# Two conditional blocks per expert pair moved ahead of the pair's own products, and one common block for all further places

## The chip, the cores and the metric

One NeuronCore of a Trainium2 chip runs the whole network in one launch. The metric is the device time of one execution in microseconds (us); less is better. Work is spread over TensorE (matrix products, PE in the profile), VectorE (DVE), ScalarE (ACT) and GpSimd (POOL); SyncE (SP) issues the loads of weights. Each engine has a sequencer of its own that takes its instructions in order, and engines wait for each other and for loads by semaphores.

## The reference

The network is two blocks of two layers each, on 256 tokens of width 1024. Twice, in the first block, a layer ends with a mixture of experts: 16 experts with a hidden width of 512, in 4 groups, of which each token takes the best two experts of the best group.

```python
h = rms_norm(x, norm2_g[layer]) * (1.0 + sc2) + sh2
x = x + g2 * grouped_moe(h, router_w, router_b, exp_w_gate[layer],
                         exp_w_up[layer], exp_w_down[layer])
```

An expert computes `(silu(h @ gate) * (h @ up)) @ down` for its tokens, weighted by the router's score. How many tokens an expert gets is known only when the router has run, so the kernel has to branch on the chip.

## The kernel before

`moe(l)` runs an expert stage, once for layer 0 and once for layer 1. It handles the experts in eight pairs, p = 0 to 7. Each expert has 64 places in its pair's own products: `up(p)` gathers the rows of its tokens with a one-hot matrix (`gather`, PE tile `ph`, evacuated by ACT into `hg`; one gather serves two pairs, so it is made in the even pairs), multiplies with the gate weights (`pg`) and the up weights (`pu`), scatters the pair before (`py`), and turns the hidden rows (`hT`, copied by DVE into `hidT`); `down(p)` multiplies with the down weights (`po`).

Tokens beyond 64 places go through `more_up` and `more_down`, 32 places of each expert at a time. Round r = 1 holds places 65 to 96 and rounds 2 to 6 the rest. The counts of a stage (`cnti`, the larger of a pair's two) are loaded into registers of PE, DVE and ACT, and `tc.If(count > ...)` makes each of them compare and branch for itself. An engine that skips a block jumps behind it and lifts the semaphores there, in EVENT_SEMAPHORE instructions, by what the skipped instructions would have lifted them.

For the pairs 2 to 6 the program reads: `up(p)`; a first block with `more_up` of round 1 and, nested in it, both halves of rounds 2 to 6; `down(p)`; a second block with `more_down` of round 1. The pair 7 has one nest in place of the first block, with all rounds for itself and for the pairs 0 and 1. Only this nest fetches weights again, so only there SP branches too; the other blocks use the weights `W` of their pair, which are still in place. With this input one block is entered: in layer 0 the first block of the pair 3 (round 1), with its second block. Everything else is skipped: in a stage five first blocks and the nest of pair 7, or in layer 0 four and the nest.

Weights come in pieces of 1 MB, twelve for a pair (four of gate, up and down each), into a ring of 17 slots (`self.turn`). SP issues them in order. A slot may be filled anew when the last instruction of the program that reads it, entered or skipped, is done. At most eight loads are under way: each one waits for the eighth before it.

The order of the instructions on each engine is made by a scheduler, but only within the stretch between two branches; the products of `gather`, `pg`, `pu` and `po` keep the order in which they are written.

Of the kernel before, what the change touches and what calls it, by code (L numbers as in the profile page):

```python
# [11 lines left out]
F32 = mybir.dt.float32  # L12
# [9 lines left out]
P = 128  # L22
D = 1024
S = 256
# [95 lines left out]
class Net:  # L120
# [1093 lines left out]
    def moe(self, l):  # L1214
# [4 lines left out]
        with self.phase(f"moe{l}", MOE_RING, True) as mp:  # L1219
# [95 lines left out]
            for p in range(FIRST):  # L1315
                V.tensor_tensor(cnt[:, 7:8], cnt[:, p:p + 1], cnt[:, 7:8], op=ALU.max)
# [42 lines left out]
            def places(oh, p, r, keep=True):  # L1359
# [7 lines left out]
                if keep:  # L1367
                    Sm = kept[:, 3 if r else 2, :]
                    ws = mp.tile([P, 1], F32, tag="ws", name="ws", bufs=3)
                else:  # L1370
                    Sm = self.sp.tile([P, 256], F32R, tag="e1", name="Sma")
                    ws = mp.tile([P, 1], F32, tag="wsa", name="wsa")
# [6 lines left out]

            def up(p, W):  # L1380

                new = p % 2 == 0
                if new:
                    hg = self.sp.tile([P, KD, 256], F32, tag="xn", name="hg", bufs=1)
                    self.first = hot((p, p + 1), 0, 64), hg
                    gather(*self.first, 0, 4)
# [22 lines left out]
                V.tensor_copy(hidT, pt)  # L1409
                return hidT, Sm, ws  # L1410
# [43 lines left out]
            def more_up(p, r, W, hidT, keep):  # L1454
# [18 lines left out]
                Sm, ws = places([twice[:, t].rearrange("p c s -> p (c s)") for t in range(2)], p, r, keep)  # L1473
# [9 lines left out]
            def more_down(p, W, hidT, Sm, ws, own=False):  # L1483
# [13 lines left out]
                if own:  # L1497
                    eh, el = (self.sp.tile([P, 512], F32R, tag="e1", name="eoa") for i in range(2))
                else:
                    eo = self.htp.tile([P, 4, 512], F32R, tag="hThi", name="eo")  # L1500
                    eh, el = eo[:, 0, :], eo[:, 1, :]
# [6 lines left out]
            def rounds(p, r, W):  # L1508

                if r < 7:  # L1510
                    with tc.If(count > 32 + 32 * r):
                        if p == 7 and r == 1:
                            self.spare = [self.slot([P, 2048]) for i in range(4)]
                        for pp, w in [(p, W)] + [(e, None) for e in range(FIRST if p == 7 else 0)]:
                            hidT = self.sp.tile([P, 4, 64], F32, tag="gt", name="hidTa")
# [821 lines left out]
```

## Time and profile before

| | |
|---|---|
| median of 3 runs | 1672.31 us (1666.22 to 1675.63) |
| profiled execution | 1670.24 us, span from first to last instruction 1668.4 us |
| granted TensorE clock, mean of the span | 0.965 |
| layer 0's experts, first gather to the end of the last `po` | 210.2 to 489.8 us |
| layer 1's experts, the same | 647.4 to 909.6 us |
| largest groups of idle PE in them | 50.8 us ahead of `po`, 6.4 us ahead of `hT` |
| weights of one stage | 96 loads of 1 MB, by SP |

The profiled execution is 2.1 us under the median of the runs; the stages lie in it at the times of the table, which count from the span's start. Within a stage the pairs follow each other in `pg`, `pu`, `hT`, `po`, and idle time of PE stands in the rows beside the group that came after it, with what ended it.

### The profile page before, as it was taken

The numbers are of one execution on the slowest core, as the hardware profiler recorded it, in microseconds if no ns is written. First come the engines' busy times: TensorE is split into PE (matmuls) and PEld (weight loads), VectorE is DVE, ScalarE is ACT, GpSimd is POOL, SyncE is SP. The second block draws the span as 40 slices with busy tenths as digits, with TensorE's granted clock in tenths as the row PEclk, the third lists the DMA queues.
The fourth block names the chain that finished last, engine by engine and source line by source line (L and its number), as shares of the span: only waits on it lengthen the run. The fifth ranks groups of instructions, "written<-read, shape, count | busy, mean of one in ns | idle before, by whom it ended". The sixth has DMA issues, their size and how long they took to land. (4 is left out here: it accounts for less than half of the span.)

```text
span 1668.4 us, 24040 instructions
## 1 busy us (share of the span) xinstructions
PE 1548.3 (93%) x9485; PEld 1109.3 (66%) x9485; DVE 855.4 (51%) x1624; ACT 651.3 (39%) x1341; POOL 123.1 (7%) x170
## 2 busy tenths in 40 slices
PE   6999999888879999998788899999999999999998
PEld 3766534333339975433233688789999897889997
DVE  4755512221238984222113776765555777755555
ACT  3435321110126553111012554664444766654443
POOL 0330200000000002000000200210000212110000
PEclk9999999998989999999899999999999999999999
DMA  9998999789977889999896743355555443454640
GB/s 358 350 315 285 367 392 354 272 303 338 344 256 231 277 317 348 397 338 384 326 340 246 230 108 94 107 183 190 190 174 172 162 135 119 143 186 158 219 155 26
DMA packets 225779, 412.58 MB, mean 247 GB/s; under 512 B 7704, under 2 KB 91312, under 8 KB 225616
## 3 DMA queue, kind: packets, MB, share of 16 engines
q1 hardware_dynamic: 223040, 403.46, 68.6%
q0 software_dynamic: 2304, 6.98, 1.3%
q8 instruction: 98, 1.61, 0.4%
q14 instruction: 65, 0.53, 0.1%
q10 hardware_dynamic: 272, 0.00, 0.0%
HBM read 409.35 MB, written 1.06 MB: 246 GB/s over the span
## 5 line engine op out<-in xcount | busy, mean ns | idle before, releaser
L229 DVE TENSOR_TENSOR hl<-w,hl 128x1024 fp32r<-128x1024 f32 x280 | 335.1, 1229 | 55.2 <-ACT hl L228 54.8
L228 ACT CAST hl<-w 128x1024 fp32r<-128x1024 f32 x280 | 280.3, 1045 | 32.0 <-DMA w<-in_even_w_in 19.8
L1427 PE MATMUL po<-w,hidT 128*64 128x512 f32 x512 | 138.0, 700 | 50.8 <-PEq L1541 21.6
L380 PE MATMUL pgu<-hThi,hl 128*128 128x256 f32 x640 | 180.9, 283 | 0.0
L382 PE MATMUL pgu<-hThi,hl 128*128 128x256 f32 x640 | 180.8, 283 | 0.0
L381 PE MATMUL pgu<-hTlo,hl 128*128 128x256 f32 x640 | 180.7, 282 | 0.0
L380 PE MATMUL lin<-hl,hThi 128*128 128x256 f32 (+2 forms) x480 | 158.6, 334 | 1.3 <-ACT hThi L551 0.6
L381 PE MATMUL lin<-hl,hThi 128*128 128x256 f32 (+2 forms) x480 | 153.2, 320 | 2.8 <-DVE hl L229 2.7
L382 PE MATMUL lin<-hl,hTlo 128*128 128x256 f32 (+2 forms) x480 | 152.6, 319 | 0.2 <-DVE hTlo L557 0.2
L1427 PEld LDWEIGHTS po<-w,hidT 128*64 128x64 f32 x512 | 45.2, 161 | 133.4 <-issue 127.7
L1396 PE MATMUL pu<-w,hg 128*64 128x512 f32 x512 | 124.6, 595 | 0.0
L381 PEld LDWEIGHTS pgu<-hTlo,hl 128*128 128x128 f32 x640 | 122.4, 191 | 1.8
L380 PEld LDWEIGHTS pgu<-hThi,hl 128*128 128x128 f32 x640 | 122.4, 191 | 1.7
L382 PEld LDWEIGHTS pgu<-hThi,hl 128*128 128x128 f32 x640 | 122.4, 191 | 0.1
L1396 PE MATMUL pg<-w,hg 128*64 128x512 f32 x512 | 115.3, 597 | 2.9 <-PEq L1545 1.7
L1442 ACT CAST eo<-of 128x512 fp32r<-128x512 f32 x32 | 19.8, 617 | 223.6 <-DVE of L1439 223.3
L380 PEld LDWEIGHTS lin<-hl,hThi 128*128 128x128 f32 x480 | 92.6, 193 | 16.3 <-issue 7.9
L1439 DVE SCALAR_TENSOR_TENSOR of<-po,ws,gate 128x512 f32<-128x512 f32 x32 | 23.9, 748 | 149.6 <-PE po L1427 149.6
L381 PEld LDWEIGHTS lin<-hl,hThi 128*128 128x128 f32 x480 | 92.5, 193 | 11.8 <-DVE hl L229 4.3
L382 PEld LDWEIGHTS lin<-hl,hTlo 128*128 128x128 f32 x480 | 92.3, 192 | 7.6 <-issue 1.7
L1417 DVE TENSOR_TENSOR x<-x,py 128x512 f32<-128x512 f32 x68 | 42.8, 683 | 99.3 <-PE py L1415 99.3
L1396 PEld LDWEIGHTS pu<-w,hg 128*64 128x64 f32 x512 | 38.2, 137 | 71.9 <-issue 70.3
(547 smaller groups left out, 2934.2 us busy)
## 6 DMA issues: line engine op xcount, KB each, us to landing
w<-in_exp_w_gate SPq DMA_DIRECT2D x64, 1024.0 KB, 16.2
w<-in_exp_w_down SPq DMA_DIRECT2D x64, 1024.0 KB, 15.4
w<-in_exp_w_up SPq DMA_DIRECT2D x64, 1024.0 KB, 10.7
w<-in_ada_w SPq DMA_DIRECT2D x48, 1024.0 KB, 7.5
w<-in_ffn_wg SPq DMA_DIRECT2D x22, 1024.0 KB, 5.5
w<-in_ffn_wu SPq DMA_DIRECT2D x22, 1024.0 KB, 7.3
w<-in_ffn_wd SPq DMA_DIRECT2D x22, 1024.0 KB, 8.8
w<-in_even_w_in SPq DMA_DIRECT2D x14, 1024.0 KB, 10.2
```

The costliest lines, as they stand in the source:

```text
L228: pin(self.nc.scalar.copy(w[:, 0], src))
L229: pin(self.nc.vector.tensor_tensor(w[:, 1], src, w[:, 0].bitcast(F32), op=ALU.subtract))
L380: pin(mm(out, lh, rh, start=start, stop=False))
L381: pin(mm(out, lh, rl, start=False, stop=False))
L382: pin(mm(out, ll, rh, start=False, stop=stop))
L1396: pin(mm(pp[64 * j:64 * j + 64, :], hg[:, k, q][:, 64 * j:64 * j + 64], w[j][k // 4][:, k % 4, :], start=k == 0, stop=k == KD - 1, tile_po ...
L1417: V.tensor_tensor(xs, xs, py, op=ALU.add)
L1427: pin(mm(po[c][64 * j:64 * j + 64, :], hidT[:, k, 64 * j:64 * j + 64], W[2][j][k // 2][:, k % 2, 512 * c:512 * c + 512], start=k == 0, sto ...
L1439: V.scalar_tensor_tensor(of, po[c], ws, gate[:, cs], op0=ALU.mult, op1=ALU.mult)
L1442: nc.scalar.copy(eh[c], of)
```

## The change

The blocks of the pairs 2 to 7 now hold round 1 alone. The first one, `more_up`, stands ahead of `up(p)` (behind `down` of the pair before), and the second one, `more_down`, between `up(p)` and `down(p)`. All rounds from 2 on, of all pairs, and round 1 of the pairs 0 and 1, form one nest ahead of the pair 7, on a count `left` that is the largest of all, with 32 added for the pairs 0 and 1. It fetches every weight itself, into the four slots that the down weights of pair 7 get after it, so those are fetched behind the nest; the first loads of the next layer follow them, ahead of the pair's own products. The gather for the next two pairs is made at the end of `up` of the pairs 1, 3 and 5 (`prepare`). `Sm` always lies in `kept` now.

```diff
@@ -1312,8 +1312,8 @@
             cnt = mp.tile([1, 8], F32, name="cnt")
             V.tensor_reduce(cnt, pc.rearrange("p (a b) -> p a b", b=2), axis=AX.X, op=ALU.max)
 
-            for p in range(FIRST):
-                V.tensor_tensor(cnt[:, 7:8], cnt[:, p:p + 1], cnt[:, 7:8], op=ALU.max)
+            V.tensor_scalar(cnt[:, 0:FIRST], cnt[:, 0:FIRST], 32.0, None, op0=ALU.add)
+            V.tensor_reduce(cnt[:, 0:1], cnt, axis=AX.X, op=ALU.max)
             cnti = mp.tile([1, 8], I32, name="cnti")
             V.tensor_copy(cnti, cnt)
 
@@ -1356,7 +1356,7 @@
                         nc.scalar.activation(hg[:, k, :], ph[:, b, :], AF.Identity,
                                              scale=A[:, k:k + 1], bias=B[:, k:k + 1])
 
-            def places(oh, p, r, keep=True):
+            def places(oh, p, r):
 
                 pS = self.bank([P, 256], name="pS")
                 pw = self.bank([P, 16], name="pw")
@@ -1364,11 +1364,10 @@
                     self.tr(pS[:, 128 * t:128 * t + 128], oh[t].bitcast(F32))
                     mm(pw, oh[t], ch[:, t, :], start=t == 0, stop=False)
                     mm(pw, oh[t], cl[:, t, :], start=False, stop=t == 1)
-                if keep:
-                    Sm = kept[:, 3 if r else 2, :]
+                Sm = kept[:, 3 if r else 2, :]
+                if not r:
                     ws = mp.tile([P, 1], F32, tag="ws", name="ws", bufs=3)
                 else:
-                    Sm = self.sp.tile([P, 256], F32R, tag="e1", name="Sma")
                     ws = mp.tile([P, 1], F32, tag="wsa", name="wsa")
                 nc.scalar.copy(Sm, pS)
                 m = 32 if r else 64
@@ -1377,13 +1376,17 @@
                     nc.scalar.copy(ws[m * i:m * i + m, :], pw[m * i:m * i + m, e:e + 1])
                 return Sm, ws
 
+            def prepare(p, k1=KD):
+
+                hg = self.sp.tile([P, KD, 256], F32, tag="xn", name="hg", bufs=1)
+                self.first = hot((p, p + 1), 0, 64), hg
+                gather(*self.first, 0, k1)
+
             def up(p, W):
 
-                new = p % 2 == 0
+                new = p == 0
                 if new:
-                    hg = self.sp.tile([P, KD, 256], F32, tag="xn", name="hg", bufs=1)
-                    self.first = hot((p, p + 1), 0, 64), hg
-                    gather(*self.first, 0, 4)
+                    prepare(0, 4)
                 oh, hg = self.first
                 q = slice(128 * (p % 2), 128 * (p % 2) + 128)
                 pg = self.bank([P, 512], name="pg")
@@ -1407,6 +1410,8 @@
                     self.tr(pt[:, k, :], hd[:, 128 * k:128 * k + 128])
                 hidT = self.sp.tile([P, 4, P], F32, tag="e2", name="hidT")
                 V.tensor_copy(hidT, pt)
+                if p in (1, 3, 5):
+                    prepare(p + 1)
                 return hidT, Sm, ws
 
             def scatter(py, t, c, Sm, eh, el):
@@ -1451,7 +1456,7 @@
                     if l:
                         self.split_ahead(PRE)
 
-            def more_up(p, r, W, hidT, keep):
+            def more_up(p, r, W, hidT):
 
 
                 oh = hot((p,), 32 + 32 * r, 32)
@@ -1470,7 +1475,7 @@
                 twice = self.sp.tile([P, 2, 2, 64], F32R, tag="gt", name="ohd")
                 for t in range(2):
                     V.tensor_copy(twice[:, t], oh[t].unsqueeze(1).to_broadcast([P, 2, 64]))
-                Sm, ws = places([twice[:, t].rearrange("p c s -> p (c s)") for t in range(2)], p, r, keep)
+                Sm, ws = places([twice[:, t].rearrange("p c s -> p (c s)") for t in range(2)], p, r)
                 hd = self.sp.tile([P, 512], F32, tag="gt", name="hda")
                 nc.scalar.copy(hd, pp)
                 pt = self.bank([P, 4, P], name="hT")
@@ -1480,7 +1485,7 @@
                 V.tensor_tensor(hidT, hidT, pt[:, :, 64:128], op=ALU.mult)
                 return Sm, ws
 
-            def more_down(p, W, hidT, Sm, ws, own=False):
+            def more_down(p, W, hidT, Sm, ws):
                 po = self.bank([P, 512], name="po")
                 w = W[2] if W else weights("exp_w_down", 256, p, self.spare)
                 for k in range(4):
@@ -1494,28 +1499,21 @@
                     h = slice(64 * c, 64 * c + 64)
                     V.scalar_tensor_tensor(of[h, :], po[h, :], ws[h, :], gate[h, 512 * c:512 * c + 512], op0=ALU.mult,
                                            op1=ALU.mult)
-                if own:
-                    eh, el = (self.sp.tile([P, 512], F32R, tag="e1", name="eoa") for i in range(2))
-                else:
-                    eo = self.htp.tile([P, 4, 512], F32R, tag="hThi", name="eo")
-                    eh, el = eo[:, 0, :], eo[:, 1, :]
+                eh, el = (self.sp.tile([P, 512], F32R, tag="e1", name="eoa") for i in range(2))
                 self.split(of, eh, el)
                 for c in range(2):
                     h = slice(64 * c, 64 * c + 64)
                     for t in range(2):
                         scatter(self.bank([P, 512], name="py"), t, c, Sm[h, 128 * t:128 * t + 128], eh[h, :], el[h, :])
 
-            def rounds(p, r, W):
-
-                if r < 7:
-                    with tc.If(count > 32 + 32 * r):
-                        if p == 7 and r == 1:
-                            self.spare = [self.slot([P, 2048]) for i in range(4)]
-                        for pp, w in [(p, W)] + [(e, None) for e in range(FIRST if p == 7 else 0)]:
-                            hidT = self.sp.tile([P, 4, 64], F32, tag="gt", name="hidTa")
-                            Sm, ws = more_up(pp, r, w, hidT, False)
-                            more_down(pp, w, hidT, Sm, ws)
-                        rounds(p, r + 1, W)
+            def rounds(r):
+
+                with tc.If(left > 32 + 32 * r):
+                    for rr, pp in [(1, e) for e in range(FIRST if r == 2 else 0)] + [(r, e) for e in range(8)]:
+                        hidT = self.sp.tile([P, 4, 64], F32, tag="e2", name="hidTa")
+                        more_down(pp, None, hidT, *more_up(pp, rr, None, hidT))
+                    if r < 6:
+                        rounds(r + 1)
 
             engines = (mybir.EngineType.PE, mybir.EngineType.DVE, mybir.EngineType.Activation)
 
@@ -1528,27 +1526,28 @@
                 return t[0::2], t[1::2]
 
             for p in range(8):
-                W = [weights("exp_w_gate", 512, p), weights("exp_w_up", 512, p), weights("exp_w_down", 256, p)]
-                if p >= FIRST:
-                    count = nc.values_load(cnti[0:1, p:p + 1], min_val=0, max_val=S,
-                                           engines=engines + (mybir.EngineType.SP,) * (p == 7))
-                own = up(p, W)
-                if p < FIRST:
-                    down(W, *own)
-                elif p < 7:
-
-                    hidT = self.sp.tile([P, 4, 64], F32, tag="e2", name="hidTb")
-                    with tc.If(count > 64):
-                        Sm, ws = more_up(p, 1, W, hidT, True)
-                        rounds(p, 2, W)
-                    down(W, *own)
-                    with tc.If(count > 64):
-                        more_down(p, W, hidT, Sm, ws, True)
-                else:
-                    rounds(p, 1, W)
+                W = [weights("exp_w_gate", 512, p), weights("exp_w_up", 512, p)]
+                self.spare = [self.slot([P, 2048]) for i in range(4)]
+                if p == 7:
+                    left = nc.values_load(cnti[0:1, 0:1], min_val=0, max_val=2 * S,
+                                          engines=engines + (mybir.EngineType.SP,))
+                    rounds(2)
+                W.append(weights("exp_w_down", 256, p, self.spare))
+                if p == 7:
                     self.turn, self.nload = [self.ring] * RING, 0
                     self.resume()
-                    down(W, *own, True)
+                if p < FIRST:
+                    down(W, *up(p, W))
+                    continue
+
+                count = nc.values_load(cnti[0:1, p:p + 1], min_val=0, max_val=S, engines=engines)
+                hidT = self.sp.tile([P, 4, 64], F32, tag="e2", name="hidTb")
+                with tc.If(count > 64):
+                    Sm, ws = more_up(p, 1, W, hidT)
+                own = up(p, W)
+                with tc.If(count > 64):
+                    more_down(p, W, hidT, Sm, ws)
+                down(W, *own, p == 7)
 
 
     def mixer1(self):
```

What the built program makes of it, engine by engine. First PE in layer 0, from the turning of pair 2's hidden rows to its second block; before, `hT` on line 183 is followed by the branch on line 1541, the last four rows of whose block (round 6) stand ahead of `po`:

```order
L1489 MATMUL po<-w,hidTa 32x512 x16
L1414 MATMUL py<-eo,Sma 128x512 x4
L1415 MATMUL py<-eo,Sma 128x512 x4
L1511 UNCONDITIONAL_BRANCH x6
L1541 UNCONDITIONAL_BRANCH
L1427 MATMUL po<-w,hidT 64x512 x16
L1545 COMPARE_AND_BRANCH
L1489 MATMUL po<-w,hidTb 32x512 x16
L1414 MATMUL py<-eoa,kept 128x512 x4
L1415 MATMUL py<-eoa,kept 128x512 x4
L1545 UNCONDITIONAL_BRANCH x2
```

and now the same place, where 1548 is the line of the second block and 1545 that of pair 3's first one:

```order
L183 MATMUL hT<-kt,hd 128x128 x4
L1548 COMPARE_AND_BRANCH
L1494 MATMUL po<-w,hidTb 32x512 x16
L1419 MATMUL py<-eoa,kept 128x512 x4
L1420 MATMUL py<-eoa,kept 128x512 x4
L1548 UNCONDITIONAL_BRANCH x2
L1432 MATMUL po<-w,hidT 64x512 x16
L1545 COMPARE_AND_BRANCH
```

The jump between `hT` and `po` skips 24 matrix instructions as these rows count them (16 + 4 + 4), where it skipped 74 + 5 x 98 = 564, and the jump behind `po` skips 74 where it skipped 24. The nest ahead of pair 7 holds 980 + 4 x 784 = 4116 (before, pair 7's held 6 x 294 = 1764).

Second, PE at pair 3 of layer 0. Before, the gather (`ph<-kept`) follows the second block of line 1545:

```order
L1427 MATMUL po<-w,hidT 64x512 x16
L1545 COMPARE_AND_BRANCH
L1489 MATMUL po<-w,hidTb 32x512 x16
L1414 MATMUL py<-eoa,kept 128x512 x4
L1415 MATMUL py<-eoa,kept 128x512 x4
L1545 UNCONDITIONAL_BRANCH x2
L1352 MATMUL ph<-kept,xh 128x256
L1352 MATMUL ph<-kept,xl 128x256
```

and now its 32 products end ahead of the second block, line 1548:

```order
L1352 MATMUL ph<-kept,xl 128x256
L1548 COMPARE_AND_BRANCH
L1494 MATMUL po<-w,hidTb 32x512 x16
L1419 MATMUL py<-eoa,kept 128x512 x4
L1420 MATMUL py<-eoa,kept 128x512 x4
L1548 UNCONDITIONAL_BRANCH x2
L1432 MATMUL po<-w,hidT 64x512 x16
L1545 COMPARE_AND_BRANCH
```

The gather moved from behind `po` to between `hT` and `po`. Third, SP's loads for pair 7 of layer 0, before:

```order
L221 DMA w<-in_exp_w_gate 128x4x512 x3
L221 DMA w<-in_exp_w_up 128x4x512
L1541 UNCONDITIONAL_BRANCH
L221 DMA w<-in_exp_w_up 128x4x512 x3
L221 DMA w<-in_exp_w_down 128x2x1024 x4
L1545 UNCONDITIONAL_BRANCH
L1511 COMPARE_AND_BRANCH
```

and now, ahead of the nest:

```order
L221 DMA w<-in_exp_w_up 128x4x512 x3
L1548 UNCONDITIONAL_BRANCH
L221 DMA w<-in_ada_w 128x4x512
L1511 COMPARE_AND_BRANCH
```

and behind it:

```order
L1511 UNCONDITIONAL_BRANCH x6
L221 DMA w<-in_exp_w_down 128x2x1024 x4
L1545 UNCONDITIONAL_BRANCH
L221 DMA w<-in_odd_w_in 128x8x256 x5
L1548 UNCONDITIONAL_BRANCH
```

The four down loads moved behind the nest, and in layer 0 one load of another weight (`ada_w`) came ahead of it.

## Rows read from the trace of the kernel before

**Rows 1.** Page, part 2: 40 slices of the span (41.7 us each), tenths.

```profile
PEclk9999999998989999999899999999999999999999
DMA  9998999789977889999896743355555443454640
```

**Rows 2.** Groups by line, PE: out<-in, count | busy us, mean ns | idle before, releasers.

```profile
L1427 PE MATMUL po<-w,hidT 128*64 128x512 f32 x512 | 138.0, 700 | 50.8 <-PEq L1541 21.6 <-DMA w<-in_exp_w_up 13.9 <-DVEq L1511 7.3
L183 PE MATMUL hT<-kt,hd 128*128 128x128 f32 x64 | 10.5, 286 | 6.4 <-DVE hd L1404 6.4
L1396 PE MATMUL pg<-w,hg 128*64 128x512 f32 x512 | 115.3, 597 | 2.9 <-PEq L1545 1.7 <-ACT hg L1356 0.7
```

**Rows 3.** Timeline of PE, pieces: start, duration, line, count, idle before and releaser.

```profile
333.36 8.78 PE L1427 MATMUL po<-w,hidT 128*64 128x512 f32 x32 [3.55 <-PEq L1511]
...
650.91 3.88 PE L1396 MATMUL pg<-w,hg 128*64 128x512 f32 x16
...
692.92 0.66 PE L183 MATMUL hT<-kt,hd 128*128 128x128 f32 x4
695.02 7.09 PE L1427 MATMUL po<-w,hidT 128*64 128x512 f32 x32 [1.44 <-DVE hidT L1409]
...
758.65 9.74 PE L1427 MATMUL po<-w,hidT 128*64 128x512 f32 x32 [5.76 <-PEq L1541]
...
867.86 9.75 PE L1427 MATMUL po<-w,hidT 128*64 128x512 f32 x32 [3.42 <-PEq L1541]
```

**Rows 4.** Sequencer instructions of line 1541: durations in ns, least/median/most.

```profile
L1541 PEldq COMPARE_BRANCH  x10: 70/3850/6242, 282.5 to 863.8; - x10
```

**Rows 5.** The same of line 1545 (second blocks).

```profile
L1545 PEldq COMPARE_BRANCH  x11: 88/237/437, 289.2 to 873.0; - x11
```

**Rows 6.** The same of line 1511 in 876:905, the nest of pair 7.

```profile
L1511 SPq EVENT_SEMAPHORE  x8: 17/17/17, 880.7 to 891.1; - x8
L1511 ACTq COMPARE_BRANCH  x1: 45/45/45, 892.9 to 892.9; - x1
L1511 ACTq EVENT_SEMAPHORE  x1: 17/17/17, 895.6 to 895.6; - x1
L1511 PEldq COMPARE_BRANCH  x1: 3492/3492/3492, 896.9 to 896.9; - x1
```

**Rows 7.** The same of line 1545 in 867:880, pair 6 of layer 1.

```profile
L1545 PEldq COMPARE_BRANCH  x1: 437/437/437, 873.0 to 873.0; - x1
...
L1545 PEldq EVENT_SEMAPHORE  x1: 51/51/51, 877.7 to 877.7; - x1
```

**Rows 8.** The same of line 1541 in 721:727, pair 2 of layer 1.

```profile
L1541 PEldq EVENT_SEMAPHORE  x1: 51/51/51, 725.3 to 725.3; - x1
```

**Rows 9.** Timeline of SP, pieces of layer 1.

```profile
725.39 2.55 SPq L221 DMA_DIRECT2D w<-in_exp_w_up  x3
...
870.40 5.02 SPq L221 DMA_DIRECT2D w<-in_exp_w_down  x4
900.58 5.22 SPq L221 DMA_DIRECT2D w<-in_ev_w_in  x5
```

**Rows 10.** Stretches of layer 1: length, busy us of each engine, clock, DMA share, GB/s.

```profile
710.00:720.00 10.00, 10.00 (x48) 3.20 (x46) 0.00 (x0) 1.57 (x4) 0.00 (x0) 1.00 1.05 387
720.00:730.00 10.00, 7.73 (x32) 4.12 (x32) 3.72 (x6) 0.58 (x3) 0.00 (x0) 0.83 0.55 181
770.00:780.00 10.00, 9.76 (x54) 4.72 (x54) 0.69 (x1) 4.19 (x9) 0.00 (x0) 1.00 1.02 408
702.00:768.50 66.50, 58.22 (x262) 24.99 (x260) 13.94 (x23) 8.63 (x20) 0.00 (x0) 0.92 0.96 353
```

**Rows 11.** Who waited for whom, SP, 870:930: us, times, longest.

```profile
SPq L1511 <- SPq L1511: 15.4, 5, 5.2
SPq L221 <- PEq L1511: 9.3, 1, 9.3
```

**Rows 12.** Instructions of line 1533, which load counts into PE's registers.

```profile
L1533 PEldq TENSOR_LOAD <-cnti x12: 294/306/487, 210.9 to 877.8; - x12
```

## Prediction

> **What bounds the kernel now.** I read the slices of the page first, then the groups by line in the two expert stages, then the timeline of PE between `hT` and `po`, the branch instructions of the sequencers, and at last SP's loads. The slices show PE's clock falling a little below full in both stages while the DMA engines are nearly, not wholly, full [rows 1]. The groups name the place: PE sits idle for 50.8 us ahead of the sixteen `po` groups, and these are busy for 138.0 us [rows 2]. A `po` group without a stall lasts 7.09 us (pair 1 of layer 1, after a wait of 1.44 us for `hidT`); pair 3's waits 5.76 us and then lasts 9.74 [rows 3]. [...] One such stretch has a granted clock of 0.83 [rows 10].
>
> The wait is a branch. PE's jump over a first block takes 3.85 us at the median and up to 6.2 [rows 4]; over a second block 0.24, at most 0.44 [rows 5]. Part of the waits is put down to a load, 13.9 us [rows 2], but DMA has pauses in these stages, and the branch alone lasts up to 6.2 us, longer than the 5.76 that are put down to it; so I count these as the branch too. DMA pauses because of the same branch: the loads of the next `up` weights go out at 725.39, as soon as PE has passed its first block at 725.3 [rows 8, 9], since that block, entered or not, is the last reader of their slots. In that stretch the load is 181 GB/s where a full one is 387 to 408 [rows 10].
>
> **The change, part by part, against the profiled 1670.24 us (2.1 us below the median of the runs).**
>
> Waits ahead of `po`. Between `hT` and `po` now stands a jump like the second block's (24 matrix instructions). Its 0.24 to 0.44 us lie inside the 1.44 us for which PE waits for `hidT` anyway; without that cover twelve would cost 5 us. After the change I count: pair 0 as now, 0.79 twice; pairs 2, 4, 6 and 7, 1.44 in both layers, 11.5; pairs 1, 3 and 5 have the gather between `hT` and `po`, which is moved and not added, so that only DVE's new one-hot rows are waited for, put at 1.0 (it lies between 0.1 and 1.44), 6.0. Sum 19.1; 50.8 - 19.1 saves **31.7 us**. The wait of 3.55 us behind the entered block of layer 0 [rows 3] is in the 50.8 and goes too, since no nested branch follows there now.
>
> Clock. No gap ahead of `po` stays above 1.44 us, and the group behind a wait of 1.44 ran at full clock [rows 3]. Saves **24.6 us**; at worst, where gaps stay between 1.5 and 2.3 us, some half of it.
>
> `hT`. In the pairs from 3 on PE waits for `hd`, since the scheduler put `py` and `pS` between the halves of `pu`. Now `pu` is whole and `py` lies behind it in all pairs, as in pair 1 before, which didn't wait [rows 3]. Of 6.4 us [rows 2] I take **5**, from 0 to 6.
>
> First blocks. Their jump (74 matrix instructions) now stands behind `po`, twelve times instead of the second block's ten. There PE's sequencer is ahead of its engine: it branched at 873.0 and its semaphore instruction came at 877.7, when `po` ended [rows 3, 7]. So 4.7 us of `po` hide a jump. Before, `pg` waited 1.7 us in all for the ten [rows 2]; I take 0.3 us each, 3.6, that is **2 lost**. The bounds: nothing, and 6.2 - 4.7 = 1.5 us each if a jump of 74 costs what the longest one does, 18. I take the short price, because 74 is nearer to 24 than to 564.
>
> [...]
>
> The nest. One jump a layer over 4116 matrix instructions, ahead of pair 7. The jump over 1764 took PE 3.5 us, and ACT got on 2.7 us after its own [rows 6]. Again `po` covers 4.7 us, less 0.3 for loading `left` [rows 12]; between 0 and 2.3 us are left over, and with half clock behind it twice that. I take 2.5 a layer, **5 lost**, from 0 to 10. DVE and ACT jump while PE has the 14 us of `pg` and `pu` ahead, which need nothing from them but evacuated banks; the next that waits for ACT is `hT`.
>
> SP and the down loads of pair 7. Behind the jump SP first waits, lane by lane, until all loads have landed (eight semaphore instructions from 880.7 to 891.1) [rows 6, 11], and the loads behind a nest wait for PE to pass it [rows 11]. So the four down loads, now issued during `po` of pair 6 (870.40), go out when that `po` has ended. They take 4 x 2.64 = 10.6 us (1.05 MB at 387 to 408 GB/s is 2.71 to 2.57 us) and up to 5.0 for issuing [rows 9, 10], 15.6. PE needs from the end of that `po` (877.6) to the branch behind `hT` (896.9) 19.3 us [rows 3, 6]: covered by 3.7. In layer 0 the load of `ada_w` ahead of the nest takes 2.6 of these. What is queued behind are the next layer's loads, which today start at 900.58, when PE has passed the nest [rows 9]; then they start after `pu` of pair 7, not later.
>
> DMA as the new bound. In layer 1 the first slots come free at 654.8 [rows 3]. The 75 loads from there to the last `up` take 75 x 2.64 = 198 us, to 853, landed by 855; the down loads 15.6 more, 871. With half of each term so far (15.9 + 12.3 + 2.5 - 1 - 2.5 = 27.2) PE ends layer 1 at 909.6 - 27.2 = 882, so `po` of pair 7 starts at 875: just behind the loads. At 2.71 us a load both come together. I take **2 lost**. The slots are free in time, because `pg` and `pu` now release them as they finish. In layer 0 PE is slower (the entered block) and has more room.
>
> The entered block of pair 3 keeps its work; it starts on DVE's rows only behind the branch: **1 lost**. The three VectorE instructions on `cnt` become two: nothing.
>
> Sum: 31.7 + 24.6 + 5 - 2 - 5 - 2 - 1 = 51.3 us: 1619 us for this execution, 1621 by the median. I say 1620.
>
> **Rivals.**
> (a) DMA bounds the stages. For it: a full stretch of one pair of pairs moves only 353 GB/s [rows 10], 2.97 us a load; if that is all it can give, the 75 loads end at 878 and `po` of pair 7 starts at 895, 20 us late, in layer 1, and some 5 late in layer 0: about 1645. Against it: that stretch contains a pause, and full stretches give 387 to 408.
> (b) The first block's jumps are long ones: 16 us less gain, and some clock with it, about 1638. Against it: the count of skipped instructions.
> (c) It is the place and not the length that makes a jump dear: at `hT` PE's queue is short, behind `po` it is long. Then the second block costs there what the first one did, waits and clock stay, and only `hT` is gained: about 1667. Against it: the durations are those of the branch itself [rows 4, 5], not of a wait behind it.
> (d) Slower: a jump's price grows with its length. 6.2 us for 564 instructions would be 45 for the 4116 of the nest, 40 not covered by `po`, in both layers 80, with the 5 taken off again: about 1695. It decides from some 30 us a nest on. Against it: 1764 instructions took 3.5 us [rows 6], less than 564 did.
>
> **How the numbers follow.** My case, 1606 to 1634, has 0.70: its ends are the best and worst of the terms on `hT` (0 to 6), the gathers' waits (plus or minus 5), the nest (0 to 10) and half of a clock loss in a few places. (a) has 0.11, (b) 0.07, (c) 0.07, (d) 0.03, and 0.02 are for others. The range 1605 to 1643 takes in (b) and half of (a). Half a per cent, about 8 us, is what a measurement of this kernel can tell from no change. Faster by more than that: my case, (a), (b) and part of the rest, 0.90; within it, (c), 0.06; slower, (d) and others, 0.04.
>
> **What will show it.** Right, if the idle time ahead of `po` falls to some 20 us and its busy time to 114, no branch but the nest's takes PE over 1 us, the clock of both stages is 1.0, loads of `up` go out as soon as `pg` ends, and the DMA digits show no pause but one at pair 7. Wrong, if `po` waits for loads (a), `pg` waits for the first block (b), the second block's branch takes PE 3 us or more (c), or `pg` of pair 7 waits for tens of us (d).

## The result

The change makes the kernel faster: 1609.39 us at the median of four runs (1609.19 to 1610.15) against 1673.91 (1666.22 to 1675.63) for the kernel before, ratio 0.9624, 95% interval 0.9593 to 0.9655. The profiled execution took 1610.15 us, span 1608.4 us, clock 0.979. From the first `pg` to the end of the last `po` layer 0 takes 250.5 us where it took 277.4, layer 1 230.2 where it took 258.7: 55.4 us of the 60.0 by which the spans differ.

The slices of the page after, each of 40.2 us: DMA stands at 8 or 9 through both expert stages, but for the slice from 442 us, where layer 0 ends.

```profile
PEclk9999999999889999999989999999999999999999
DMA  9988999989958899999998541646544542636540
```

The groups of PE after, columns as in [rows 2]:

```profile
L1432 PE MATMUL po<-w,hidT 128*64 128x512 f32 x512 | 113.9, 597 | 9.4 <-DVEq L1548 5.8 <-DVE hidT L1412 1.6 <-ACT hg L1356 1.2
L183 PE MATMUL hT<-kt,hd 128*128 128x128 f32 x64 | 10.5, 286 | 0.4 <-DVE hd L1407 0.4
L1399 PE MATMUL pg<-w,hg 128*64 128x512 f32 x512 | 117.6, 611 | 19.9 <-ACTq L1545 9.3 <-DVEq L1511 7.9 <-PEq L1545 2.8
L1399 PE MATMUL pu<-w,hg 128*64 128x512 f32 x512 | 115.3, 593 | 2.8 <-DMA w<-in_exp_w_up 2.8
L1352 PE MATMUL ph<-kept,xh 128*128 128x256 f32 x128 | 33.0, 297 | 2.9 <-DVE kept L1340 2.9
```

Against [rows 2] the wait ahead of `po` has gone from 50.8 to 9.4 us, its busy time from 138.0 to 113.9, and `hT` waits 0.4 us where it waited 6.4. Against that, `pg` waits 19.9 us where it waited 2.9, and 17.2 of them are put down to the sequencers of ACT and DVE. The row of `pu` before, not shown so far, is this:

```profile
L1396 PE MATMUL pu<-w,hg 128*64 128x512 f32 x512 | 124.6, 595 | 0.0
```

So `pu` is busy for 9.3 us less, with the same instructions of the same length. Before, most pairs had it in pieces with `py` between them (in pair 4 of layer 1, 16, 2 and 14 products at 780.1, 785.0 and 787.3 us); now it runs whole. The timeline of PE after shows a usual pair (3 and 4 of layer 1) and `pg` of pair 7 in either layer:

```profile
724.89 7.09 PE L1432 MATMUL po<-w,hidT 128*64 128x512 f32 x32 [0.41 <-ACT hg L1356]
732.29 7.09 PE L1399 MATMUL pg<-w,hg 128*64 128x512 f32 x32 [0.30 <-PEq L1545]
739.17 7.07 PE L1399 MATMUL pu<-w,hg 128*64 128x512 f32 x32
750.17 7.09 PE L1432 MATMUL po<-w,hidT 128*64 128x512 f32 x32 [0.83 <-DVEq L1548]
...
436.34 9.30 PE L1399 MATMUL pg<-w,hg 128*64 128x512 f32 x32 [7.85 <-DVEq L1511]
...
826.52 8.77 PE L1399 MATMUL pg<-w,hg 128*64 128x512 f32 x32 [9.25 <-ACTq L1545]
```

A usual pair has only waits under 1 us. The one gap is ahead of pair 7, behind the nest: 17.1 us in the two layers, and `pg` lasts 2.21 and 1.68 us longer than 7.09, because the clock has fallen (0.50 from 436.3 to 440.0 in layer 0, and 0.50 in the stretch from 820 to 830 in layer 1). That makes 21.0 us in all. The sequencers at the nest (line 1511) and at the first block behind it (1545) in layer 0:

```profile
L1511 PEldq COMPARE_BRANCH  x1: 6261/6261/6261, 424.4 to 424.4; - x1
...
L1511 ACTq COMPARE_BRANCH  x1: 45/45/45, 430.0 to 430.0; - x1
L1511 DVEq COMPARE_BRANCH  x1: 56/56/56, 430.7 to 430.7; - x1
L1511 PEldq EVENT_SEMAPHORE  x1: 51/51/51, 430.8 to 430.8; - x1
L1511 ACTq EVENT_SEMAPHORE  x1: 17/17/17, 435.3 to 435.3; - x1
L1511 DVEq EVENT_SEMAPHORE  x1: 21/21/21, 436.1 to 436.1; - x1
...
L1545 PEldq COMPARE_BRANCH  x1: 4384/4384/4384, 431.0 to 431.0; - x1
```

PE jumps from 424.4 to 430.7 us, most of it while `po` of pair 6 runs (421.4 to 428.5). ACT and DVE come to the nest, at 430.0 and 430.7, only when they have evacuated that `po` (DVE's last read of it ends at 429.7), and their semaphore instructions behind it follow 5.3 and 5.4 us after the branch (6.8 and 6.7 in layer 1). PE meanwhile stands in a second jump, over 74 instructions, which takes 4.4 us here, against 0.35 at the median of the thirteen; in layer 1 it takes 0.25, and `pg` still starts 6.4 us after PE is through, just behind ACT and DVE.

### The profile page after: what moved, and what is told of

Its sections match the earlier page's. It is cut to its first block, busy times and chain, and to the rows that moved or that the text cites. A ratio compares the mean times of both kernels' runs of the same rounds, so it can differ in the third digit from the quotient of the medians.

```text
span 1608.4 us, 24108 instructions
## 1 busy us (share of the span) xinstructions
PE 1511.7 (94%) x9485; PEld 1107.2 (69%) x9485; DVE 855.1 (53%) x1624; ACT 650.3 (40%) x1341; POOL 121.7 (8%) x170
## 5 line engine op out<-in xcount | busy, mean ns | idle before, releaser
L1399 PE MATMUL pg<-w,hg 128*64 128x512 f32 x512 | 117.6, 611 | 19.9 <-ACTq L1545 9.3
L1407 DVE TENSOR_TENSOR hd<-hd,pu 128x512 f32<-128x512 f32 x16 | 11.0, 687 | 226.5 <-PE pu L1399 226.5
L1432 PE MATMUL po<-w,hidT 128*64 128x512 f32 x512 | 113.9, 597 | 9.4 <-DVEq L1548 5.8
L1399 PE MATMUL pu<-w,hg 128*64 128x512 f32 x512 | 115.3, 593 | 2.8 <-DMA w<-in_exp_w_up 2.8
L1399 PEld LDWEIGHTS pg<-w,hg 128*64 128x64 f32 x512 | 40.7, 141 | 92.8 <-issue 68.7
L1432 PEld LDWEIGHTS po<-w,hidT 128*64 128x64 f32 x512 | 40.2, 138 | 72.9 <-issue 59.3
L2222 ACT ACTIVATE g<-g 128x256 f32<-128x256 f32 x40 | 16.8, 420 | 162.7 <-DVE g L2221 162.7
```

Source lines behind the costliest of these rows:

```text
L1399: pin(mm(pp[64 * j:64 * j + 64, :], hg[:, k, q][:, 64 * j:64 * j + 64], w[j][k // 4][:, k % 4, :], start=k == 0, stop=k == KD - 1, tile_po ...
L1407: V.tensor_tensor(hd, hd, pu, op=ALU.mult)
L1432: pin(mm(po[c][64 * j:64 * j + 64, :], hidT[:, k, 64 * j:64 * j + 64], W[2][j][k // 2][:, k % 2, 512 * c:512 * c + 512], start=k == 0, sto ...
L2222: Sc.activation(g, g, AF.Silu)
```

## The experiments

Theory: the gap is three jumps. PE's own is mostly covered by `po`; PE's second one follows at once; and ACT and DVE have to pass the nest before `pg` gets its PSUM bank, since the nest uses all eight banks of the pool `ps` and lifts their semaphores only then. Rivals: PE's own jump alone, or a load at the end of the stage.

| run | median us | ratio to before, 95% | layer 0 + layer 1, us |
|---|---|---|---|
| changed kernel | 1609.4 | 0.9593 to 0.9655 | 250.5 + 230.2 |
| short blocks, old place | 1620.2 | 0.9656 to 0.9705 | 255.9 + 234.2 |
| long blocks, new place | 1646.3 | 0.9817 to 0.9863 | 273.8 + 243.3 |
| the same, own banks | 1630.1 | 0.9723 to 0.9760 | 264.6 + 236.9 |
| gather back | 1613.9 | 0.9618 to 0.9666 | 253.8 + 229.9 |
| no nest | 1593.5 | 0.9487 to 0.9534 | 240.8 + 225.0 |
| nest of one round | 1607.5 | 0.9565 to 0.9617 | 250.4 + 227.4 |
| nest behind `hT` of pair 7 | 1612.8 | 0.9610 to 0.9658 | 249.5 + 234.2 |
| blocks of pair 7 late | 1617.6 | 0.9649 to 0.9692 | 250.4 + 230.2 |
| the same, nest with own banks | 1610.5 | 0.9605 to 0.9646 | 244.8 + 230.0 |
| own banks, pair 7 in the nest | 1605.6 | 0.9592 to 0.9630 | 244.5 + 227.9 |
| the same, loads ahead of the nest | 1601.4 | 0.9560 to 0.9597 | 244.4 + 226.2 |
| changed kernel again | 1609.3 | 0.9595 to 0.9625 | 250.6 + 229.9 |

The last column is read from the timeline of PE, in one profiled execution of each run; the two of the changed kernel agree to 0.3 us in the sum. The stretch between the layers (158.7 to 162.6 us) and the one behind them (752.6 to 758.6) differ from run to run by up to 4 and 6 us though no edit touches them, so the layers tell more than the medians.

**Length or place of a block.**

```diff
+                own = up(p, W)
                 hidT = self.sp.tile([P, 4, 64], F32, tag="e2", name="hidTb")
                 with tc.If(count > 64):
                     Sm, ws = more_up(p, 1, W, hidT)
-                own = up(p, W)
+                if p < 7:
+                    down(W, *own)
                 with tc.If(count > 64):
                     more_down(p, W, hidT, Sm, ws)
-                down(W, *own, p == 7)
+                if p == 7:
+                    down(W, *own, True)
```

> The two short blocks go back to the places that the conditional blocks had in the kernel before (the first behind hT, the second behind po); the nest for all further places stays ahead of pair 7. Theory, it is the length of a block that makes its jump dear: a jump over 74 matrix instructions behind hT takes PE 0.3 to 0.4 us, po's idle time stays under 30 us and its busy time at 114 to 118, and what is lost is only that the slots of gate and up are released some 15 us later, at the first block's jump: 1609 to 1630 us, 1616 the likeliest. Rival (c) of the prediction, it is the place: behind hT the jump takes 3 us or more as before, po's idle time goes back to some 45 us with busy time near 135, about 1655 us.

1620.2 us. The first block's jump behind `hT` takes 0.32 us where it took 3.85 [rows 4], and `po` waits hardly longer than in the changed kernel (9.9 us against 9.4):

```profile
L1546 PEldq COMPARE_BRANCH  x13: 70/318/441, 281.8 to 852.0; - x13
```

```profile
L1432 PE MATMUL po<-w,hidT 128*64 128x512 f32 x512 | 115.1, 602 | 9.9 <-DVEq L1546 4.3 <-DVE hidT L1412 3.3 <-ACTq L1546 1.3
L1399 PE MATMUL pu<-w,hg 128*64 128x512 f32 x512 | 123.2, 594 | 0.0
L183 PE MATMUL hT<-kt,hd 128*128 128x128 f32 x64 | 10.5, 286 | 8.1 <-DVE hd L1407 8.1
```

It is the length. The loss of 9 us in the layers is not that of late slots (`pu` waits for no load): `pu` is at 123.2 us again, and `hT` waits 8.1 us. So the place of the block is what gave `pu` its 9 us and `hT` its 6; why the scheduler leaves `pu` whole there was not tested.

**Long blocks at the new place**, as the prediction costed them. `further` nests the rounds 2 to 6 of the pair, with the weights `W` in place; the rest of the edit gives these blocks tiles of their own and leaves only the pairs 0 and 1 in the nest.

```diff
...
                 with tc.If(count > 64):
                     Sm, ws = more_up(p, 1, W, hidT)
+                    further(p, 2, W, t)
```

> The first blocks stay where the change has them, ahead of each pair's own products, but hold the further rounds of their pair in nested blocks again, some 370 matrix instructions instead of 74; the nest ahead of pair 7 keeps the rounds of pairs 0 and 1, and the rounds 2 to 6 of pair 7 are in its own first block. Nothing is left out. The prediction's step for a long jump behind po: 4.7 us of po cover it, 0 to 1.5 us each for twelve: 1609 to 1627 us. Theory after the runs so far: pg also waits for VectorE and ScalarE, which reach the block only when po has been evacuated, and pass it some 3 to 5.5 us later, since the block uses all banks: some 5 to 7 us ahead of pg in each of twelve pairs, with half clock behind: 1670 us (1645 to 1700).

1646.3 us. The block has 564 matrix instructions (74, and five rounds of 98; the 370 above were miscounted). `pg` waits 47.5 us in all. A pair with 2.9 us, and its sequencers:

```profile
703.30 8.78 PE L1401 MATMUL pg<-w,hg 128*64 128x512 f32 x32 [2.88 <-DVEq L1555]
```

```profile
L1555 PEldq COMPARE_BRANCH  x1: 6112/6112/6112, 696.0 to 696.0; - x1
...
L1555 PEldq EVENT_SEMAPHORE  x1: 51/51/51, 702.2 to 702.2; - x1
...
L1555 DVEq COMPARE_BRANCH  x1: 63/63/63, 702.7 to 702.7; - x1
L1555 DVEq EVENT_SEMAPHORE  x1: 21/21/21, 703.0 to 703.0; - x1
```

PE is through at 702.2, DVE comes last to the block, at 702.7, and passes it in 0.3 us; `pg` starts at 703.3. So the theory's wait for DVE is there, but it is 1 us a pair where I had expected 3 us or more: DVE's part of this block is short. Pair 7 waits 8.7 and 8.3 us, since two long jumps follow each other there.

Then the same with five PSUM banks for these blocks and the nest (the edit to `bank` is shown below):

> As the run with the long first blocks at the new place, but these blocks, and the nest, take their PSUM tiles from five banks that pg and pu of the pair do not get. Nothing is left out. Theory, of the 47.5 us ahead of pg in that run some 44 were waits for VectorE and ScalarE to pass the block; with the banks apart only PE's own jump is left, 6.0 us at the median less the 4.4 us that po covers, some 1.6 us in each of twelve pairs, 19 us, and the half clock goes: 1612 us (1605 to 1620). Rival, the wait for VectorE and ScalarE is for something else than the bank and stays, or goes over to pu: 1640 us or more.

1630.1 us, neither figure. In the pairs 2 to 6, but for the entered block, `pg` now waits 0.3 to 2.05 us, behind PE's own jump, and the granted clock is 1.00; pair 7 waits as long as ever, for PE alone:

```profile
780.56 7.09 PE L1406 MATMUL pg<-w,hg 128*64 128x512 f32 x32 [2.04 <-PEq L1563]
...
847.67 8.98 PE L1406 MATMUL pg<-w,hg 128*64 128x512 f32 x32 [10.34 <-PEq L1563]
```

So the bank is what `pg` waited for beyond PE's own jump, some 1 us a pair. What the expectation missed is that two jumps in a row are both paid (6.0 and 6.4 us in layer 0, 6.2 and 7.6 in layer 1), since `po` covers only the first.

**The gather.** `prepare(p + 1)` at the end of the odd pairs' `up` is taken out, and the even pairs gather for themselves again.

> The gather of a pair of pairs goes back into the even pair's up, as in the kernel before; all else as in the changed kernel. The prediction counted the moved gather at nothing but a wait of 1.0 us for its one-hot rows: 1609 us, plus or minus 3. Theory with a gain in the move: behind po of the odd pair PE then waits for VectorE's one-hot rows and ScalarE's copies ahead of pg, where now po and hT of the odd pair cover them: 2 to 3 us in each of six pairs: 1620 to 1627 us. Rival, the gather covers the short first block's jump of its pair and nothing else: 1605 us.

1613.9 us, 3.0 us more in the layers: the move is worth a little, more than the prediction's nothing and less than the second theory said. By the medians alone the two kernels can't be told apart, since the intervals overlap. `po` waits 15.4 us in place of 9.4, because the gather no longer stands between `hT` and `po` in the odd pairs; `ph` waits 1.0 in place of 2.9, and its two groups are busy for 66.7 us in place of 64.4.

**The nest: taken out, shortened, moved.**

```diff
-                    left = nc.values_load(cnti[0:1, 0:1], min_val=0, max_val=2 * S,
-                                          engines=engines + (mybir.EngineType.SP,))
-                    rounds(2)
+                    pass
```

> The nest ahead of pair 7 is taken out; it left out further rounds 2 to 6 of all pairs and round 1 of pairs 0 and 1, none of which this input enters. Theory, the gap of pair 7 is the jumps of all three engines over the nest: the 7.9 and 9.3 us ahead of pg and the 2.2 and 1.7 us by which pg is longer go, 21 us in the two layers: 1588 us (1584 to 1593). Rival, the prediction's own 2.5 us a layer was right for the nest and the rest of the gap is a load or another wait at the end of a stage, which stays: 1604 us (1599 to 1609).

1593.5 us: the nest costs 16 us by the medians, 14.9 in the layers.

```profile
L1399 PE MATMUL pg<-w,hg 128*64 128x512 f32 x512 | 114.8, 595 | 5.1 <-PEq L1543 3.5 <-DMA w<-in_exp_w_gate 1.6
L1399 PE MATMUL pu<-w,hg 128*64 128x512 f32 x512 | 116.1, 593 | 5.4 <-DMA w<-in_exp_w_up 5.4
```

Of the 21.0 us, 17.6 are off `pg` (14.8 of waiting, 2.8 of length); loads take some back, 7.0 us of waiting for DMA in `pg` and `pu` where it was 2.8.

```diff
-                    if r < 6:
+                    if r < 2:
                         rounds(r + 1)
```

> The nest holds round 2 (and round 1 of pairs 0 and 1) only; rounds 3 to 6, which this input does not enter, are left out. PE still jumps over some 980 matrix instructions, VectorE over 121 and ScalarE over 161. Theory, pg of pair 7 waits for VectorE and ScalarE, whose jumps come behind PE's and get short here: the gap falls to some 2 us a layer, which is PE's own jump of 3.5 to 6.3 us less the 4.4 us that po covers: 1593 us (1590 to 1599). Rival, PE's jump sets the gap, whatever its length beyond a few hundred instructions, and the other two only follow: the gap stays at 7 to 9 us: 1606 us (1602 to 1611).

1607.5 us, the rival's time, but not by its reason. In layer 0:

```profile
L1511 PEldq COMPARE_BRANCH  x1: 6196/6196/6196, 426.5 to 426.5; - x1
...
L1511 ACTq COMPARE_BRANCH  x1: 45/45/45, 432.1 to 432.1; - x1
...
L1511 DVEq COMPARE_BRANCH  x1: 56/56/56, 432.9 to 432.9; - x1
L1511 DVEq EVENT_SEMAPHORE  x1: 21/21/21, 433.4 to 433.4; - x1
L1511 ACTq EVENT_SEMAPHORE  x1: 17/17/17, 437.7 to 437.7; - x1
...
L1545 PEldq COMPARE_BRANCH  x1: 4542/4542/4542, 432.9 to 432.9; - x1
```

DVE now passes 120 instructions in 0.5 us, but ACT still needs 5.6 for 160, and PE's second jump takes 4.5 (5.9 in layer 1). Two of the three are left, and either is enough: in layer 0 PE is through its second jump at 437.5 us and ACT through the nest at 437.7.

In the next run the nest stands between `hT` and `po` of pair 7.

> The nest moves from ahead of pair 7 to between hT and po of pair 7, with the slots of gate of pair 7 as its own, and the down loads of pair 7 are issued without waiting for it. Theory, VectorE and ScalarE have nothing to give PE there but the evacuation of po, so that they jump beside PE: one bare jump of PE, 6.3 us, and half clock behind it, some 3 us, in each layer in place of the 10.5 us now: 1606 us (1602 to 1611). Rival, the loads of the stage behind, which now go out ahead of pg of pair 7, wait on SP until PE has passed the nest, some 35 us later, and the DMA engines stand still meanwhile: 10 to 30 us lost: 1620 to 1640 us.

1612.8 us, a little over the theory's range. `po` of pair 7 waits 7.8 and 7.3 us for PE's bare jump, as the theory said. In layer 1 `pg` and `pu` wait for loads, up to 1.6 us at a time and 7.3 us in all, but they do so with no nest too (7.0 us), so this is not the rival's wait behind the nest.

**The three jumps one by one.** First the blocks of pair 7 behind its `up`, then also five banks for the nest:

```diff
-        t = self.ps.tile([P, 512], dt, tag="bk", name=name)
+        if self.own:
+            t = self.own[0]
+            self.own = self.own[1:] + [t]
+        else:
+            t = self.ps.tile([P, 512], dt, tag="bk", name=name)
...
+                    self.own = [self.ps.tile([P, 512], F32, tag="bk", name="nest") for i in range(5)]
                     rounds(2)
+                    self.own = []
...
+                if p == 7:
+                    own = up(p, W)
                 with tc.If(count > 64):
                     Sm, ws = more_up(p, 1, W, hidT)
-                own = up(p, W)
+                if p < 7:
+                    own = up(p, W)
```

> Only the second half of that edit: pair 7 makes its own products ahead of its two short blocks, the nest uses the common banks as in the changed kernel. Theory, VectorE and ScalarE still have to pass the nest before pg of pair 7 has its bank; they came at 435 to 436 us and 826 us in the changed kernel, where pg began at 436.3 and 826.5, so the gap stays at 7 to 9 us: 1608 us (1604 to 1612). Rival, PE's own two jumps in a row set the gap, and without the second one it falls to some 3 us: 1597 us.

1617.6 us, slower than expected, though the layers are unchanged; the loss lies in the stretches outside them and stays open. With PE's second jump out of the way the gap is still 17.6 us, now all for DVE at the nest:

```profile
L1399 PE MATMUL pg<-w,hg 128*64 128x512 f32 x512 | 117.8, 611 | 20.4 <-DVEq L1511 17.6 <-PEq L1547 2.8
```

> Nothing of the computation is left out. The nest takes its PSUM tiles from five banks of its own, so that pg of pair 7 gets a bank that the nest does not use, and pair 7 makes its own products ahead of its two short blocks, so that no second jump of PE stands right behind the nest's. Theory, pg of pair 7 waits in series: for PE's jump over the nest, for a second jump right behind it, and for VectorE and ScalarE to pass the nest, because they release its bank. With the last two gone, PE's own 6.2 us less the 4.4 us that po covers are left, some 2 us a layer, and pg runs at full clock: 1594 us (1590 to 1599). Rival, the bank is not what PE waits for, or pu then waits for VectorE instead: the gap moves to pu or stays: 1604 us or more.

With the banks apart, the one difference from the run before, the gap falls as the theory said, in both layers, though ACT and DVE pass the nest no earlier (435.9 and 436.7 in layer 0):

```profile
431.10 8.63 PE L1404 MATMUL pg<-w,hg 128*64 128x512 f32 x32 [2.48 <-PEq L1516]
...
816.74 8.67 PE L1404 MATMUL pg<-w,hg 128*64 128x512 f32 x32 [2.61 <-PEq L1516]
...
831.17 3.65 PE L1404 MATMUL pu<-w,hg 128*64 128x512 f32 x14 [1.49 <-SPq L1516]
...
846.44 3.65 PE L1437 MATMUL po<-w,hidT 128*64 128x512 f32 x14 [1.86 <-DMA w<-in_exp_w_down]
```

Against the expectation, `pg` of pair 7 does not run at full clock: 0.81 was granted while it ran. Still 1610.5 us: the mechanism is right and the time wrong. Layer 0 gains 5.6 us, layer 1 nothing, because there `pu` and `po` of pair 7 now wait for loads, one of them for SP at the nest; what the stretches outside the layers lose stays open, as before. In the two layers together the gain is 5.8 us, from a block that is not entered and now keeps to five of the eight banks.

So the last step also handles round 1 of pair 7 in the nest and lets it load into four slots of its own, behind the down weights of pair 7:

```diff
-                    for rr, pp in [(1, e) for e in range(FIRST if r == 2 else 0)] + [(r, e) for e in range(8)]:
+                    for rr, pp in [(1, e) for e in (0, 1, 7) if r == 2] + [(r, e) for e in range(8)]:
...
-                self.spare = [self.slot([P, 2048]) for i in range(4)]
+                W.append(weights("exp_w_down", 256, p))
                 if p == 7:
+                    self.spare = [self.slot([P, 2048]) for i in range(4)]
...
-                W.append(weights("exp_w_down", 256, p, self.spare))
```

> Nothing of the computation is left out. Three edits to the changed kernel: the nest has five PSUM banks of its own; round 1 of pair 7 is handled in the nest as that of pairs 0 and 1, so that pair 7 has no block of its own and PE no second jump behind the nest's; and the nest loads into four slots taken behind the down weights of pair 7, so that SP issues these loads ahead of the nest. Theory, the run with own banks took the wait for VectorE and ScalarE away (2.5 us ahead of pg of pair 7 in place of 8 and 9) and gave it back to loads of pair 7 that SP held behind the nest, and to the start of the stages behind; here the layers take 244.5 and 226 us and the stages behind as in the changed kernel: 1599 us (1595 to 1603). Rival, the DMA engines are full at the end of a layer whatever SP does, and the loads come when they came: 1608 us (1604 to 1612).

> As the run with the nest apart, but the nest loads into the slots of the down weights of pair 7 again, as in the changed kernel, so that SP issues these loads behind the nest. Nothing is left out. Theory, with SP's loads behind the nest the stall that PE loses ahead of pg comes back ahead of pu and po of pair 7, in layer 1 above all (230 us as in the changed kernel): 1605 us (1602 to 1609). Rival, it was the late blocks of pair 7 that lost the time in the run with own banks, and not SP: 1599 us, the same as with the nest apart.

1601.4 us with all of it, 1605.6 without the loads' part. Both lie where the theories said, but the 4 us between them are less than the scatter of either (8 and 10 us), and in the layers the loads' part is worth 1.8 us, all in layer 1; so the theory on SP is not shown to be right. In the first, SP issues the down loads of pair 7 at 423.2 us in layer 0, ahead of the nest, where the changed kernel issues them at 435.8. `pg` waits 8.0 us in all:

```profile
L1405 PE MATMUL pg<-w,hg 128*64 128x512 f32 x512 | 117.1, 608 | 8.0 <-PEq L1517 5.2 <-PEq L1553 2.9
```

> The changed kernel once more, unedited, with more rounds than its first timing, to set the run with the nest apart (1601 us, 0.9579 of the kernel before) against it. If the nest's place, banks and loads are worth what the two layers show, 10 us, this run stays at 1609 us (1607 to 1612), ratio 0.961 to 0.963; if the run with the nest apart was fast by the scatter of executions alone, this one comes to 1601 to 1605 us as well.

1609.3 us, so the version with the nest apart beats the changed kernel by 8 us at the median and by 10 in the layers; the two intervals just touch. Little is left to gain in layer 1: its loads run at 385 to 406 GB/s from 640 to 820 us (385 to 408 in the changed kernel), and it takes 226.2 us where it takes 225.0 with no nest at all. That the loads hold it is argued from these figures; no run here changed them alone. Layer 0 takes 244.4 us, 3.6 more than with no nest.

## Why the prediction was right, and where it was not

The forecast of 1619 us for this execution came out at 1610.15. By its steps:

- Waits ahead of `po`, 31.7: 41.4, less 2.5 more ahead of `ph` (0.4 before). The second block's jump does lie inside the wait for `hidT`, which is 0.83 and not 1.44 us; the gather's pairs wait some 0.5 ahead of `ph` and at most 0.4 ahead of `po`, rather than 1.0.
- Clock, 24.6, which is 138.0 less sixteen times 7.09 us [rows 2, 3]: 24.1. Before, `po` of pair 3 in layer 1, behind its wait of 5.76 us, had a granted clock of 0.50 from 758.65 to 764 us and of 1.00 from there to its end. Now a `po` lasts 7.09 us everywhere but behind the entered block (7.60).
- `hT`, 5: 6.0. First blocks: 0.30 to 0.34 us each, as put, 1.1 more in all than the second blocks before. DMA, 2: 2.8. The entered block, 1: `ph` there waits 1.9 us longer.
- Not in the sum: `pu`, 9.3 gained. That `py` no longer cuts it in two was said under `hT`, but only the wait was priced.
- **The nest, 5, with 10 as its bound: 21.0** by the rows, 14.9 in the layers once it is gone. This is the step that failed: "DVE and ACT jump while PE has the 14 us of `pg` and `pu` ahead, which need nothing from them but evacuated banks". The banks are those of the nest itself. ACT and DVE gave them back only behind the nest, with semaphore instructions 5.3 to 6.8 us after their branches (the last at 436.1 and 826.2 us, and `pg` began at 436.34 and 826.52), and they reach it only behind `po` of pair 6. Own banks took that wait away, from 7.85 and 9.25 us to 2.5 and 2.6: in layer 0 `pg` then began at 431.1 us, ahead of ACT's and DVE's semaphores (435.9 and 436.7). The second jump of PE behind the first had not been seen either. PE's own jump was sized well: 6.2 us, 2.5 to 2.7 of them bare.

The sum of these is 51.5 against 51.3: the nest's cost, put 16 us too low, and the gains of `po` and `pu`, put 16 us too low as well, cancel. That the sum came out is luck. A further 4 us were gained in the layers. Most of it stands in the rows of `pg` and `ph`: without the 3.9 us by which the low clock lengthens it in pair 7 `pg` is busy for 113.7 us where it was 115.3, and `ph` for 64.4 where it was 66.7, since the gather no longer cuts `pg` in two; the prediction put this move at nothing but waits. The last 5 us lie in the stretches outside the layers, which no edit touches and which differ by as much between runs. Of the signs that the prediction named, one failed: a branch besides the nest's took PE 4.4 us, the one right behind it.

Rival (b), long jumps over the first blocks, falls with the 0.30 to 0.34 us. Rival (c), place and not length, falls with the short blocks at the old place. Rival (d), a price that grows with length, falls with the rows: on PE 24 instructions cost 0.2 us and 74 mostly 0.3; 564 cost 3.85 at the median before [rows 4] and 6.0 at the new place, 1764 3.5 [rows 6], and 980 and 4116 mostly 6.2. A long block cost more than a short one here, but among the long ones the price did not grow. Where between 74 and 564 instructions the price goes up, and why 74 cost some 4 us in a few places, no run here shows. That each engine pays for itself is what the nest showed (in layer 0 PE 6.3 us, ACT 5.3, DVE 5.4). Rival (a) holds in part: in layer 1 the DMA runs at 385 to 408 GB/s from 640 to 820 us, and `pu` of its pairs 5 and 6 waits 2.8 us for loads.

## What to carry to other kernels

A conditional block that was skipped here cost its jump on every engine that had a part in it, and each engine jumped only when it got there (at the nest of layer 0 PE at 424.4 us, for 6.3, ACT at 430.0, for 5.3, and DVE at 430.7, for 5.4): look for the one that comes last, and for what it must hand back. Give a block that is rarely entered PSUM banks that the next hot instruction doesn't use (the waits ahead of `pg` of pair 7 fell from 17.6 to 5.1 us), and keep one jump from following a long one (right behind the nest 74 instructions cost 4.4 us in layer 0, though 0.25 in layer 1). Issuing the next loads ahead of the block was worth 1.8 us here, which is not clear of the scatter. When a stall is taken away beside a nearly full DMA (385 to 408 GB/s in layer 1), expect part of it back: of the 21.0 us here, taking the nest out gained 14.9 in the layers, and own banks, which took 13 of them away by the rows, gained 5.9.

## What was unexpected of the hardware

- A jump over 74 matrix instructions mostly costs PE 0.3 us, but right behind a long jump 4.4 and 4.5 us in layer 0 of two runs of the changed kernel and 0.25 us in layer 1 of both; 4.5 and 5.9 with the nest of one round. In six other versions it took 3.8 to 4.1 us in single pairs of layer 1 with no long jump just before it (3.90 and 3.77 us ahead of the pairs 4 and 5 with no nest), and `po` covered it. In the two runs of one kernel it went with the place in the program and not with the execution; what it is about the place stays open.
- ACT passed blocks of 95 instructions in 0.5 us, but right behind the nest in 4.5 and 4.7 (long blocks with own banks); one of 160 took it 5.4 and 5.6, the full nest (672) 4.5 to 6.8. DVE passed 120 in 0.5 and the full nest (504) in 4.4 to 6.7.
- `pg` behind a wait of 2.5 to 3.1 us lasted 8.6 to 8.8 us in some pairs (granted clock 0.80 to 0.82 meanwhile) and 7.09 in others (clock 1.00, behind 2.86, 3.07, 3.08 and 3.11 us). What decides between the two, these rows don't show.
